# In each MLP's second pair, one block's products a step later; new issue times around both attention stages

## The chip, the cores and the metric

The kernel runs on one core of a Trainium2 chip. The metric is the device time of one execution in microseconds (us); the median of repeated runs counts. The engines are TensorE (PE; its weight loads are listed as PEld), VectorE (DVE), ScalarE (ACT), GpSimd (POOL) and SyncE (SP). SP computes nothing here: it issues DMAs, in the order in which they are written. POOL issues some DMAs too.

## What is computed

The reference is a trunk of two layers over 256 tokens of width 2048, all in float32. The parts that matter here:

```python
h = x
# layer A
u = rms_norm(h, a_norm_g);  q, k, v, fz = split(u @ a_w_in)     # 2048 x (3*2048 + 16)
h = h + forgetting_attention(norm(q), norm(k), v, log_sigmoid(fz + b_f)) @ a_w_out
h = h + relu(rms_norm(h, g) @ mlp_w1[0])**2 @ mlp_w2[0]         # 2048 x 8192, 8192 x 2048
# keys and values shared by the B layers, then layer B
k_sh, v_sh = split(rms_norm(h, kv_norm_g) @ kv_w)
q = norm(rms_norm(h, b_norm_g) @ b_w_q)
h = h + chunked_relbias_attention(q, norm(k_sh), v_sh, rel) @ b_w_out
h = h + relu(rms_norm(h, g) @ mlp_w1[1])**2 @ mlp_w2[1]
```

## The kernel before

**Products.** Nearly all time goes into products with weights. Every float32 weight block is split on the chip into a high part `hi` (a rounding copy on ACT, line 312) and a low part `lo` (a subtraction on DVE, line 313). A product of 512 columns is then three matmuls on PE: high by high (line 579), high weights by the low part of the activations (line 581), low weights by high (line 583). The third pass is the first that needs `lo`.

**Pairs, forms and own units.** The weights are cut into pairs. A pair has four corner blocks, "11", "12", "21" and "22", and instead of eight block products does seven, of the sums that Strassen's scheme wants. The program calls each of the seven a form; in order they are "11", T3 = 22 + 12, T2 = T3 + 11, T1 = 12 + 11, "21", T4 = T2 + 21, and "22". A form of the MLPs has two halves of 6 matmuls each. What the scheme leaves over are own units (`a2` to `a7`, `b2` to `b7`), ordinary pieces of weights with 12 matmuls each.

**Where the sums are made.** T3 and T2 are additions on DVE (`make`, line 937), each in two halves. T1 and T4 are accumulating DMAs issued by POOL (`put`, line 946): the new block is added in memory to a tile that holds the other term. `bring` (line 911, SP) loads the corner blocks. Tiles are named after what they hold: `raw` and `zraw` are pieces for own units, `w` a loaded corner of an MLP pair, `wT` the tile for T3, T2 and T4 in turn, `R` corners in the attention stages, `query` the T3 of the query projection.

**What sets the order.** The instruction order on each engine is the order of the program text; nothing reorders it. `TABLES["ORD"]` says for each kind of pair how own units and the last forms alternate after the first four forms: in "a4 F F a5 a6 a7 F b4" the three F are forms "21", T4 and "22" (that the fifth, sixth and seventh come in this order is `FO`, "456"). Tables with six entries (`W1F`, `W2F`, `QF` and so on) say how many own units ahead of a pair's start its loads of "12", "22", "21", "11" and its T3 and T1 are issued:

```python
for name, at in zip(("12", "22", "21", "11", "T3", "T1"), p.units):
    if d == at and p.deep and name == "T3":
        make(p, "T3", 0)
    elif d == at:
        (bring if name[0] != "T" else put if p.adds and name == "T1" else make)(p, name)
```

The second half of T3 follows one own unit later. `fetch` lets ACT and DVE split up to three units ahead of PE. Side work (softmax pieces, squares, sums, transposes, copies of rows) sits in a list of steps, `fill`; masks such as `HM` and `KM` say how many steps run after each unit of the attention stages, and `ATA`, `ATB`, `LONG`, `SHORT`, `KX`, `XOH`, `T0H` and the like into which step each piece is put.

**Ways of turning a result.** The output of a product is turned for the next one: DVE transposes 32 by 32 blocks into `z` (line 427), and then either `hop` copies 16 small blocks, eight DMAs on SP and eight on POOL (line 453, `q<-z`), or `carry` writes whole rows to DRAM (line 437, `turn<-z`) and reads them back with four DMAs (line 443, `q<-turn`). Of the tables `T`, `T0H` and `T0K` an entry of -1 in second place means `hop`.

**The order of stages.** Projection of layer A with its attention woven in, output projection, MLP A, which ends with the pairs of the query projection (`in_w_qb`, tables `QF` and `QS`), key and value projection with attention B, output projection, MLP B. In each MLP the pairs of the first matrix (`in_w1fa`, `in_w1fb`) and of the second (`in_w2fa`, `in_w2fb`) alternate after the first two; the "second pair" is the second of the first matrix, and a pair of the second matrix follows it.

Of the kernel before, what the change touches and what calls it, by code (L numbers as in the profile page):

```python
# [27 lines left out]
UN = 1024  # L28
AHEAD = 2
TABLES = {  # L30
    "ATA": ((11, 13, 15, 19, 10), (9, 12, 16, 18, 10), (8, 13, 15, 19, 9), (9, 9, 12, 12, 10)),
    "ATB": ((10, 13, 14, 18, 9), (9, 13, 15, 16, 11), (10, 12, 15, 17, 10), (7, 10, 12, 12, 9)),
# [13 lines left out]
    "LONG": ((0, 1, 2, 5, 9, 11, 11, 14, 14), (0, 0, 0, 4, 7, 9), (1, 0, 1, 3, 5, 5), (2, 0, 1, 2, 4, 5)),  # L46
    "OFH": (12, 8, 2, 7, 5, 5),
    "OFK": (11, 10, 5, 6, 8, 4),
    "ORD": {"deep1": "a4 F b4 F a5 F a6 a7", "qkv": "a2 a3 a4 F a5 F a6 F a7 b2 b3 b4", "ahead0": "F a4 F a5 a6 a7 F b4",
        "kv": "a2 F a3 a4 a5 F a6 a7 F b2 b3 b4", "deep0": "a4 F F F b4 a5 a6 a7", "ahead1": "a4 F F a5 a6 a7 F b4"},  # L50
    "OSH": (10, 11, 5, 6, 4, 2),
    "OSK": (8, 8, 6, 7, 4, 2),
    "OUTH": "F a2 a3 a4 a5 F b2 b3 F b4 G b5 G a6 a7 G b6 b7 G c2 G c3 G c4 c5 G c6 c7 d2 d3 d4",
    "OUTK": "a2 a3 F b2 a4 b3 F a5 F b4 b5 G G a6 a7 G b6 G c2 b7 G c3 G c4 c5 d2 G c6 c7 d3 d4",
    "QF": (4, 7, 1, 4, 2, 2),
    "QS": (10, 5, 4, 8, 3, 1),
    "SHORT": ((2, 0, 1, 4, 7, 7, 9, 9, 12), (2, 2, 3, 3, 7, 7, 8, 11, 13), (0, 1, 1, 4, 7, 7), (0, 0, 0, 2, 4, 4)),
# [13 lines left out]
    "XOH": (9, 12, 13, 10),  # L71
    "XOK": (9, 14, 12, 14),
    "XS": (2, 5, 4, 1),
}
EARLY = 3
LAZY = ("qkv", "kv", "out0", "out1")
# [3 lines left out]
DEEP = 2 * UN  # L80
WIDE1 = (1, 2, 3, 4, 5, 6, 7)
# [15 lines left out]
def trunk(ctx: ExitStack, tc: tile.TileContext, xT, xr, gs, hg, bf, wgate, w_in, w_oa, w1a, w1fa, w1sa, w2fa, w2sa,  # L97
          w_kv, w_qb, w_ob, w1b, w1fb, w1sb, w2fb, w2sb, rel, out):
    nc = tc.nc
    V, S, G, TE, SY = nc.vector, nc.scalar, nc.gpsimd, nc.tensor, nc.sync  # L100

    def pool(name, bufs, **kw):
        return ctx.enter_context(tc.tile_pool(name=name, bufs=bufs, **kw))
# [5 lines left out]
    qkv = pool("qkv", 2)  # L109
# [82 lines left out]
    def plan_mlp(w1, w1f, w1s, w2f, w2s, rest, when, more=None):  # L192
        pairs = []

        def add(w, wf, ws, i, wides, order, times, cols=WIDE):
            j = wides.index(i) if i in wides else i - sum(1 for k in wides if k < i)
            names = ("11", "12", "21", "22")
            if i in wides:
                m = 8 - cols // 512
                src = [[None] * (8 - m) + [ws[m * (2 * j + q) + u] for u in range(m)] for q in range(2)]  # L200
                big = {k: wf[4 * j + m] for m, k in enumerate(names)}
            else:
                src = [[w[16 * j + 8 * q + u] for u in range(8)] for q in range(2)]
                big = {k: src[int(k[1]) - 1][int(k[0]) - 1] for k in names}
            pairs.append(Pair(big, src, order, len(pairs) % 2 == 1, times, cols if i in wides else UN))

        rooms = {"12": "v0", "22": "k0", "11": "k1", "21": "v1"}
        seq = [(0, 0, 0), (0, 0, 1)]
        for c in range(NCH):
            seq += [(1, c, 0)] + [(0, c + 1, 0)] * (c + 1 < NCH) + [(1, c, 1)] + [(0, c + 1, 1)] * (c + 1 < NCH)  # L210
        for m, (second, c, q) in enumerate(seq):
            i = 2 * c + q
            if second:
                add(None, w2f, w2s, i, WIDE2, "deep%d" % q, TABLES["W2L" if i == 7 else "W2S" if q else "W2F"], DEEP)
            else:
                add(w1, w1f, w1s, i, WIDE1, "ahead%d" % q if i else "early", TABLES["W1E" + when] if not i else TABLES["W1I" + when] if i == 1 else TABLES["W1S" if q else "W1F"], DEEP)
            pairs[-1].at = second, c, q
        if more is not None:
            for q in range(2):
                add(more, None, None, q, (), "" if q else "query", TABLES["QS" if q else "QF"])  # L220
                pairs[-1].at = 1, NCH, q
        plan, rest = join(pairs, rooms, rest)
        return queue(plan + rest)

    def queue(plan):
        units.extend(Form(p, i, q == 3) if q > 1 else p.src[q][i] for p, q, i in plan)
        return plan

    def join(pairs, rooms, rest):
        plan = []  # L230
        for p in pairs:
            p.rooms = rooms
            if p.order != "early":
                rooms = {"12": rooms["11"], "22": rooms["12"], "11": rooms["21"], "21": rooms["22"]}
            mine, rest = p.plan(rest)
            plan += mine
        return plan, rest
# [33 lines left out]

    plan_h, rest, tail_h = plan_heads(w_in, "H", w_oa)
    plan_a = plan_mlp(w1a, w1fa, w1sa, w2fa, w2sa, rest, "H", w_qb)
    plan_k, rest, tail_k = plan_heads(w_kv, "K", w_ob)
    plan_b = plan_mlp(w1b, w1fb, w1sb, w2fb, w2sb, rest, "K")
    ready = deque()

# [118 lines left out]
    def room(tag, name, dtype=F32):  # L396
        return qkv.tile([P, DEEP], dtype, name=name, tag=tag, bufs=1)
# [72 lines left out]
    LONG, SHORT, SHORT2 = TABLES["LONG"], TABLES["SHORT"], TABLES["SHORT2"]  # L470
# [351 lines left out]
    early = room("bias", "early")  # L822
# [521 lines left out]
```

## Time and profile before

| | us |
|---|---|
| Median of 3 runs | 2069.12 |
| Lowest, highest | 2067.84, 2071.15 |
| The profiled execution | 2071.87 |
| Its span | 2070.1 |
| PE busy | 2050.1 (99%) |
| DVE busy | 1776.8 (86%) |
| ACT busy | 1398.8 (68%) |
| POOL busy | 243.9 (12%) |

PE executes 9068 matmuls. Times in the views are those of the one profiled execution, counted from the start of its span. In a timeline a row has the start, the duration, the engine, the line, the operation, output and inputs, how many instructions it groups, and in brackets how long the engine stood idle before it and what ended that. Instructions of one engine overlap a little, so that the distance of two starts is less than a duration.

### The profile page before, as it was taken

The numbers are of one execution on the slowest core, as the hardware profiler recorded it, in microseconds if no ns is written. First come the engines' busy times: TensorE is split into PE (matmuls) and PEld (weight loads), VectorE is DVE, ScalarE is ACT, GpSimd is POOL, SyncE is SP. The second block draws the span as 40 slices with busy tenths as digits, with TensorE's granted clock in tenths as the row PEclk, the third lists the DMA queues.
The fourth block names the chain that finished last, engine by engine and source line by source line (L and its number), as shares of the span: only waits on it lengthen the run. The fifth ranks groups of instructions, "written<-read, shape, count | busy, mean of one in ns | idle before, by whom it ended". The sixth has DMA issues, their size and how long they took to land.

```text
span 2070.1 us, 27097 instructions
## 1 busy us (share of the span) xinstructions
PE 2050.1 (99%) x9068; PEld 1689.7 (82%) x9068; DVE 1776.8 (86%) x2058; ACT 1398.8 (68%) x1799; POOL 243.9 (12%) x355
## 2 busy tenths in 40 slices
PE   9999999999999999999999999999999999999999
PEld 7888878878888888888888888888788888888887
DVE  6788788889899899899888678888998988988996
ACT  6766566667677677676778566667766675776764
POOL 1111010021101102101012011100211111111020
PEclk9999999999999999999999999999999999999999
DMA  9898888788889898897988888888888888888885
GB/s 328 258 278 273 265 262 268 281 263 256 284 270 284 252 299 274 243 286 251 285 253 262 290 260 265 256 264 284 277 284 270 267 267 286 259 284 260 288 261 148
DMA packets 174221, 556.20 MB, mean 269 GB/s; under 512 B 40688, under 2 KB 68992, under 8 KB 151040
## 3 DMA queue, kind: packets, MB, share of 16 engines
q1 hardware_dynamic: 153344, 463.94, 62.8%
q0 software_dynamic: 20448, 89.96, 21.9%
q8 instruction: 71, 1.16, 0.2%
q14 instruction: 70, 0.57, 0.1%
q10 hardware_dynamic: 288, 0.57, 0.1%
HBM read 514.50 MB, written 26.76 MB: 261 GB/s over the span
## 4 chain that ended last, share of the span: by engine, by line
PE 82%; DMA 6%; issue 5%; DVE 4%; ACT 1%; SPq 1%; POOL 0%; DVEq 0%; ACTq 0%; POOLq 0%
PE acc L579 19%; PE acc L583 19%; PE acc L581 19%; PE s L583 7%; PE s L579 7%; PE s L581 7%; DVE lo L313 2%; DMA wT<-in_w1fa 2%; ACT hi L312 1%; DMA raw<-in_w_in 1%; PE po L751 1%; DMA wT<-in_w1fb 1%; PE po L714 1%; DMA w<-in_w2fb 1%; DMA turn<-z 0%
## 5 line engine op out<-in xcount | busy, mean ns | idle before, releaser
L313 DVE TENSOR_TENSOR lo<-raw,hi 128x1024 fp32r<-128x1024 f32 (+1 forms) x414 | 500.0, 1212 | 94.6 <-ACT hi L312 86.2
L312 ACT ACTIVATE hi<-raw 128x1024 fp32r<-128x1024 f32 (+1 forms) x414 | 434.7, 1054 | 198.1 <-PE acc L581 134.2
L579 PE MATMUL acc<-hi,act 128*128 128x512 f32 x1784 | 500.1, 393 | 8.1 <-ACT hi L312 7.6
L583 PE MATMUL acc<-lo,act 128*128 128x512 f32 x1784 | 494.4, 390 | 1.3 <-DVE lo L313 1.0
L581 PE MATMUL acc<-hi,act 128*128 128x512 f32 x1784 | 493.8, 390 | 0.0
L579 PEld LDWEIGHTS acc<-hi,act 128*128 128x128 f32 x1784 | 333.4, 188 | 79.3 <-ACT hi L312 10.1
L583 PEld LDWEIGHTS acc<-lo,act 128*128 128x128 f32 x1784 | 334.1, 188 | 74.8 <-DVE lo L313 5.9
L581 PEld LDWEIGHTS acc<-hi,act 128*128 128x128 f32 x1784 | 335.3, 188 | 70.7 <-DVE act L370 0.5
L312 ACT ACTIVATE hi<-w 128x1024 fp32r<-128x1024 f32 x258 | 271.1, 1058 | 127.9 <-PE acc L581 86.5
L313 DVE TENSOR_TENSOR lo<-wT,hi 128x1024 fp32r<-128x1024 f32 x220 | 267.1, 1221 | 74.7 <-ACT hi L312 71.0
L313 DVE TENSOR_TENSOR lo<-w,hi 128x1024 fp32r<-128x1024 f32 x258 | 310.0, 1217 | 20.1 <-ACT hi L312 18.8
L312 ACT ACTIVATE hi<-wT 128x1024 fp32r<-128x1024 f32 x220 | 232.2, 1059 | 114.1 <-PE acc L581 51.8
L579 PE MATMUL s<-hi,act 128*128 128x512 f32 x530 | 146.4, 391 | 0.0
L583 PE MATMUL s<-lo,act 128*128 128x512 f32 x530 | 145.3, 389 | 0.7 <-DVE lo L313 0.7
L581 PE MATMUL s<-hi,act 128*128 128x512 f32 x530 | 144.8, 388 | 0.0
L453 POOL DMA_DIRECT2D q<-z x200 | 99.4, 512 | 251.8 <-DVE z L427 212.0
L583 PEld LDWEIGHTS s<-lo,act 128*128 128x128 f32 x530 | 99.0, 188 | 22.6 <-DVE lo L313 2.4
L581 PEld LDWEIGHTS s<-hi,act 128*128 128x128 f32 x530 | 99.4, 188 | 20.6
L579 PEld LDWEIGHTS s<-hi,act 128*128 128x128 f32 x530 | 99.1, 188 | 20.8 <-ACT hi L312 0.4
L579 PE MATMUL s<-hi,S 128*128 128x512 f32 x288 | 89.5, 392 | 0.0
L583 PE MATMUL s<-lo,S 128*128 128x512 f32 x288 | 88.9, 390 | 0.1
L581 PE MATMUL s<-hi,S 128*128 128x512 f32 x288 | 88.7, 389 | 0.0
(213 smaller groups left out, 2235.8 us busy)
## 6 DMA issues: line engine op xcount, KB each, us to landing
raw<-in_w_in SPq DMA_DIRECT2D x75, 512.0 KB, 5.8
w<-in_w2fa SPq DMA_DIRECT2D x32, 1024.0 KB, 6.4
w<-in_w2fb SPq DMA_DIRECT2D x32, 1024.0 KB, 6.2
w<-in_w1fa SPq DMA_DIRECT2D x28, 1024.0 KB, 7.2
w<-in_w1fb SPq DMA_DIRECT2D x28, 1024.0 KB, 7.0
raw<-in_w2sa SPq DMA_DIRECT2D x52, 512.0 KB, 7.7
raw<-in_w_kv SPq DMA_DIRECT2D x52, 512.0 KB, 5.2
raw<-in_w2sb SPq DMA_DIRECT2D x51, 512.0 KB, 7.0
```

The source lines that it names most:

```text
L312: S.activation(hi[:, c], raw[:, c], AF.Copy)
L313: V.tensor_tensor(lo[:, c], raw[:, c], hi[:, c].bitcast(F32), op=ALU.subtract)
L453: (G if i % 2 else SY).dma_start(dst[32 * j : 32 * j + 32, i * n : (i + 1) * n], z[32 * i : 32 * i + 32, j * n : (j + 1) * n])
L579: TE.matmul(ps[:, cols], xh, cut(hi, j), start=first, stop=False, **kw)
L581: TE.matmul(ps[:, cols], xl, cut(hi, j), start=False, stop=False, **kw)
L583: TE.matmul(ps[:, cols], xh, cut(lo, j), start=False, stop=last, **kw)
L714: TE.matmul(s[:, P : 3 * P], q[:, a, P:T], k[:, a], start=True, stop=True)
L751: TE.matmul(po[:, :T], v[:, 0, a * P : (a + 1) * P], pT[:, :2], start=True, stop=False)
```

## The change

The kind of the second pair changes from "ahead1" to a kind of its own, "second". The fifth own unit, `a5`, comes between form "21" and form T4 there, so T4's products are 12 matmuls later in PE's order. The tables for the attention stages, the pairs right behind them and the query projection get other numbers. The number of matmuls, splits and loads stays; one of the turned results (third entry of `T0K`) goes by `carry` instead of `hop`.

```diff
-        "kv": "a2 F a3 a4 a5 F a6 a7 F b2 b3 b4", "deep0": "a4 F F F b4 a5 a6 a7", "ahead1": "a4 F F a5 a6 a7 F b4"},
+        "second": "a4 F a5 F a6 a7 F b4"},
...
-    "QF": (4, 7, 1, 4, 2, 2),
+    "QF": (4, 4, 2, 3, 2, 1),
...
-    "W1IH": (11, 7, 6, 7, 3, 2),
+    "W1IH": (11, 7, 6, 9, 4, 1),
...
-                add(w1, w1f, w1s, i, WIDE1, "ahead%d" % q if i else "early", TABLES["W1E" + when] if not i else TABLES["W1I" + when] if i == 1 else TABLES["W1S" if q else "W1F"], DEEP)
+                add(w1, w1f, w1s, i, WIDE1, ("second" if i == 1 else "ahead%d" % q) if i else "early", TABLES["W1E" + when] if not i else TABLES["W1I" + when] if i == 1 else TABLES["W1S" if q else "W1F"], DEEP)
```

Because of one line more at the top of the file, line numbers after the change are higher by one.

On DVE, in MLP A's second pair, before: `wT_3816` holds T4, the `raw`, `zraw` and `raw` that follow it are `a5`, `a6` and `a7`; `wT_4141` is T3 of the next pair, `w_4071` and `w_4001` are that pair's "22" and "12", and `w_3713` is the second pair's "22".

```order
L313 TENSOR_TENSOR lo<-wT_3816,hi 128x1024 x2
L313 TENSOR_TENSOR lo<-raw,hi 128x1024
L313 TENSOR_TENSOR lo<-zraw,hi 128x1024
L313 TENSOR_TENSOR lo<-raw,hi 128x1024
L937 TENSOR_TENSOR wT_4141<-w_4071,w_4001 128x1024
L313 TENSOR_TENSOR lo<-w_3713,hi 128x1024
```

The same place after (T4 is now in `wT_3798`, the next pair's T3 in `wT_4113`, the second pair's "22" in `w_3715`):

```order
L314 TENSOR_TENSOR lo<-raw,hi 128x1024
L314 TENSOR_TENSOR lo<-wT_3798,hi 128x1024 x2
L938 TENSOR_TENSOR wT_4113<-w_4071,w_4001 128x1024
L314 TENSOR_TENSOR lo<-zraw,hi 128x1024
L314 TENSOR_TENSOR lo<-raw,hi 128x1024
L314 TENSOR_TENSOR lo<-w_3715,hi 128x1024
```

The subtraction for `a5` now stands ahead of T4's two, and the first half of the next pair's T3 stands right behind them, ahead of the subtractions for `a6` and `a7` instead of behind them. MLP B has the same order at its second pair.

On SP, at the end of MLP A, before: `w_8744`, `w_8883` and `w_8885` are "22", "12" and "11" of the first pair of the query projection.

```order
L437 DMA turn<-z 128x1024
L911 DMA w_8744<-in_w_qb 128x1024
L291 DMA raw<-in_w2sa 128x1024
L443 DMA q<-turn 32x4x256 x4
L291 DMA raw<-in_w2sa 128x1024
L437 DMA turn<-z 128x1024
L291 DMA zraw<-in_w2sa 128x1024
L911 DMA w_8883<-in_w_qb 128x1024
L911 DMA w_8885<-in_w_qb 128x1024
L291 DMA raw<-in_w2sa 128x1024
L443 DMA q<-turn 32x4x256 x4
```

The same place after: `w_8881` and `w_8883` are "12" and "22", `w_8939` is "11".

```order
L438 DMA turn<-z 128x1024
L292 DMA zraw<-in_w2sa 128x1024
L912 DMA w_8881<-in_w_qb 128x1024
L912 DMA w_8883<-in_w_qb 128x1024
L292 DMA raw<-in_w2sa 128x1024
L444 DMA q<-turn 32x4x256 x4
L912 DMA w_8939<-in_w_qb 128x1024
```

"22" is now issued with "12", and "11" stands behind the four reads of `turn`, which were behind it.

On DVE, in attention A near the start of the kernel, before: `row`, `pbuf` and `t` belong to the softmax, and `acc<-acc,p_980` combines two accumulators of a pair.

```order
L734 RECIPROCAL row<-row 128x2
L736 TENSOR_SCALAR pbuf<-pbuf,row 128x128
L736 TENSOR_SCALAR pbuf<-pbuf,row 128x256
L427 STREAM_TRANSPOSE pbuf<-pbuf 128x3x4x32
L723 SCALAR_TENSOR_TENSOR t<-po,cq,nb 128x128
L725 TENSOR_REDUCE row<-t 128x1
L723 SCALAR_TENSOR_TENSOR t<-po,cq,nb 128x256
L725 TENSOR_REDUCE row<-t 128x1
L976 SCALAR_TENSOR_TENSOR acc<-acc,p_980 128x512
L313 TENSOR_TENSOR lo<-R,hi 128x1024
```

The same place after:

```order
L977 SCALAR_TENSOR_TENSOR acc<-acc,p_980 128x512
L314 TENSOR_TENSOR lo<-R,hi 128x1024
L735 RECIPROCAL row<-row 128x2
L737 TENSOR_SCALAR pbuf<-pbuf,row 128x128
L737 TENSOR_SCALAR pbuf<-pbuf,row 128x256
L428 STREAM_TRANSPOSE pbuf<-pbuf 128x3x4x32
L724 SCALAR_TENSOR_TENSOR t<-po,cq,nb 128x128
L726 TENSOR_REDUCE row<-t 128x1
L724 SCALAR_TENSOR_TENSOR t<-po,cq,nb 128x256
L726 TENSOR_REDUCE row<-t 128x1
```

The combining step and the split of the next `R` now come ahead of the eight softmax instructions. Some 150 us later, also in attention A, the first addition for T3 of a pair (`wT<-R`) stands four subtractions earlier.

More of the change, by code (lines that the diff above doesn't have):

```diff
@@ L30 @@
 TABLES = {
-    "ATA": ((11, 13, 15, 19, 10), (9, 12, 16, 18, 10), (8, 13, 15, 19, 9), (9, 9, 12, 12, 10)),
-    "ATB": ((10, 13, 14, 18, 9), (9, 13, 15, 16, 11), (10, 12, 15, 17, 10), (7, 10, 12, 12, 9)),
[1 row of a table removed]
+    "ATA": ((11, 13, 15, 19, 9), (9, 12, 16, 18, 11), (8, 13, 15, 19, 9), (9, 9, 12, 12, 10)),
+    "ATB": ((10, 13, 14, 18, 9), (9, 13, 15, 17, 11), (9, 12, 15, 17, 10), (7, 10, 12, 12, 9)),
[1 row of a table added]
     "GS": (1,),
[11 rows of a table removed]
[L46 to L49, printed above, removed]
-        "kv": "a2 F a3 a4 a5 F a6 a7 F b2 b3 b4", "deep0": "a4 F F F b4 a5 a6 a7", "ahead1": "a4 F F a5 a6 a7 F b4"},
[L51 to L54, printed above, removed]
-    "QF": (4, 7, 1, 4, 2, 2),
-    "QS": (10, 5, 4, 8, 3, 1),
-    "SHORT": ((2, 0, 1, 4, 7, 7, 9, 9, 12), (2, 2, 3, 3, 7, 7, 8, 11, 13), (0, 1, 1, 4, 7, 7), (0, 0, 0, 2, 4, 4)),
[1 row of a table removed]
[11 rows of a table added]
+    "LONG": ((0, 1, 2, 5, 9, 10, 11, 14, 14), (0, 0, 0, 4, 7, 9), (1, 0, 1, 2, 5, 5), (1, 0, 1, 4, 5, 5)),
+    "OFH": (11, 10, 1, 7, 7, 7),
+    "OFK": (10, 9, 4, 9, 8, 4),
[3 rows of a table added]
+    "OSH": (7, 9, 7, 5, 5, 1),
+    "OSK": (9, 7, 4, 7, 5, 1),
+    "OUTH": "F a2 a3 b2 a4 a5 b3 b4 F G F G b5 a6 a7 G b6 b7 G c2 G c3 G d2 c4 c5 G c6 c7 d3 d4",
+    "OUTK": "a2 a3 F b2 a4 F b3 a5 F b4 b5 G G a6 a7 G b6 G c2 b7 d2 G c3 G c4 c5 c6 G c7 d3 d4",
+    "QF": (4, 4, 2, 3, 2, 1),
+    "QS": (10, 4, 4, 8, 3, 1),
+    "SHORT": ((4, 0, 0, 3, 6, 8, 8, 9, 12), (2, 2, 3, 3, 7, 7, 8, 10, 13), (2, 0, 0, 2, 6, 7), (0, 0, 0, 2, 4, 5)),
[1 row of a table added]
     "T": ((1, -1, 5, 14, 14, 14, 15, 20, 20), (0, 2, 8, 10, 10, 14, 18, 20, 22), (0, -1, 5, 6, 7, 7), (0, -1, 4, 5, 5, 5)),
[4 rows of a table removed]
[4 rows of a table added]
     "W1F": (7, 5, 1, 5, 4, 3),
[2 rows of a table removed]
[2 rows of a table added]
     "W1S": (8, 6, 4, 5, 4, 1),
     "W2F": (6, 5, 1, 5, 4, 3),
[1 row of a table removed]
[1 row of a table added]
     "W2S": (7, 7, 4, 5, 3, 1),
-    "XOH": (9, 12, 13, 10),
+    "XOH": (9, 12, 13, 11),
     "XOK": (9, 14, 12, 14),
-    "XS": (2, 5, 4, 1),
+    "XS": (0, 5, 6, 2),
 }
```

38 rows, old and new, of the table TABLES are left out of this document.

## The prediction

> **What bounds the kernel now.** I read the busy times first, then what PE waited for, then the timelines around each wait. The first row is from the page, the others from the waits of PE (total us, times, longest us).
>
> ```profile
> PE 2050.1 (99%) x9068; PEld 1689.7 (82%) x9068; DVE 1776.8 (86%) x2058; ACT 1398.8 (68%) x1799; POOL 243.9 (12%) x355
> PE acc L579 <- ACT hi L312: 7.6, 6, 3.4
> PE acc L583 <- DVE lo L313: 2.6, 3, 1.2
> ```
>
> PE sets the end, and a change that keeps all matmuls can win only PE's waits (2070.1 - 2050.1, 20 us at most, the start included) and slow matmuls. The longest wait, 3.4 us, is at T4 of MLP A's second pair. PE's timeline there, then its clock, then two pieces of the chain of waits:
>
> ```profile
> 442.21 0.92 PE L579 MATMUL acc<-hi,act 128*128 128x512 f32 x2 [3.37 <-ACT hi L312]
> 446.65 1.09 PE L579 MATMUL acc<-hi,act 128*128 128x512 f32 x4
> ```
>
> ```profile
> 400.00:450.00 50.00, 46.58 (x196) 37.23 (x195) 39.11 (x40) 32.12 (x37) 9.74 (x18) 0.97 0.88 287
> ```
>
> ```profile
> 448.65 0.91 PE acc L583 x4
> 468.68 0.73 PE acc L583 x2
> ```
>
> Four matmuls take 0.91 us later on, 0.2275 each, so the two halves of T4, 12 matmuls, should take 2.73. From 442.21 to 446.65 they take 4.44: after the wait they run slowly, at a cost of 1.71, and the granted clock (0.97) is the trace of it. Wait and slowness make 5.08 us. ACT was waiting for POOL's accumulating DMA; POOL's and ACT's rows:
>
> ```profile
> 426.83 0.92 POOL L946 DMA_DIRECT2D wT<-in_w1fa  x1 [2.69 <-DVE lo L313]
> 441.10 2.01 ACT L312 ACTIVATE hi<-wT 128x1024 fp32r<-128x1024 f32 x2 [4.48 <-DMA wT<-in_w1fa]
> ```
>
> MLP B has the same place, with less of it and no slow matmuls behind it:
>
> ```profile
> 1465.34 0.73 PE L579 MATMUL acc<-hi,act 128*128 128x512 f32 x2 [1.18 <-ACT hi L312]
> 1481.81 1.20 PE L583 MATMUL s<-lo,act 128*128 128x512 f32 x4 [0.37 <-DVE lo L313]
> ```
>
> **The second pair of MLP A.** The put's place does not move, so T4 is ready at 442.21 again. PE is free at 442.21 - 3.37 = 438.84, does `a5` until 441.57, and waits 0.64 instead of 3.37; the slow stretch goes. Gross, 5.08 - 0.64 = 4.4 us.
>
> What is late next is the following pair. Its T3 now stands on DVE directly behind T4's two subtractions, and needs that pair's "22", which SP issues only behind a hop. SP's rows, and the landing of the loads in both MLPs (first A, then B):
>
> ```profile
> 431.61 10.69 SPq L453 DMA_DIRECT2D q<-z  x8
> 442.41 1.00 SPq L911 DMA_DIRECT2D w<-in_w2fa  x2
> DMA to landing us min/median/max: 4.9/5.8/6.7
> ```
>
> ```profile
> 1464.44 0.83 SPq L911 DMA_DIRECT2D w<-in_w2fb  x2
> DMA to landing us min/median/max: 5.0/6.0/7.0
> ```
>
> And DVE's timeline in MLP A:
>
> ```profile
> 442.19 2.36 DVE L313 TENSOR_TENSOR lo<-wT,hi 128x1024 fp32r<-128x1024 f32 x2 [2.84 <-ACT hi L312]
> 444.47 1.22 DVE L313 TENSOR_TENSOR lo<-raw,hi 128x1024 fp32r<-128x1024 f32 x1
> ...
> 448.62 1.22 DVE L937 TENSOR_TENSOR wT<-w,w 128x1024 f32<-128x1024 f32 x1
> ...
> 452.51 1.23 DVE L313 TENSOR_TENSOR lo<-w,hi 128x1024 fp32r<-128x1024 f32 x1 [0.36 <-ACT hi L312]
> ...
> 458.94 1.23 DVE L313 TENSOR_TENSOR lo<-w,hi 128x1024 fp32r<-128x1024 f32 x1 [0.53 <-ACT hi L312]
> ...
> 467.41 1.22 DVE L313 TENSOR_TENSOR lo<-wT,hi 128x1024 fp32r<-128x1024 f32 x1
> ```
>
> Before, "22" lands at 442.41 + 4.9 = 447.3 and T3 starts at 448.62, 1.3 later: it waits for nothing. After, DVE is through with T4 at 444.47 and stands 2.8 us until 447.3. Behind it are queued the subtractions for `a6` and `a7` and all else on DVE. A subtraction occupies 1.14 (two from 442.19 to 444.47), T3's half as much, so `a6` has its `lo` at about 447.35 + 2.3 = 449.6. PE comes out of T4 at 441.57 + 0.64 + 2.73 = 444.94 and does the 8 matmuls of `a6` that need no `lo` (1.82) until 446.8: it waits 2.8 to 2.9. So much of the 4.4 is gone again.
>
> The rest goes to DVE itself. T3 starts 1.27 earlier than before, but two subtractions (2.28) that stood ahead of it now stand behind it, so that DVE is 1.0 later from there on. Two gaps of before, 0.36 and 0.53, fill up. At 467.41 DVE is where it was, 0.1 later; and at 468.68 PE's third pass starts as soon as this `lo` is there. Whatever PE has won since 442 is lost there. Net: 0, with bounds of -0.5 (another such gap does not fill) and +2.8 (no wait for "22").
>
> Whether the new wait makes matmuls slow again can be read between two rows: 3.37 did, 1.18 did not, and 2.85 is nearer the first. By the row, up to 1.7 us of slowness at `a6`. The Trainium skill ("TensorE: Matmul & The Clock Gate", Part 1, What's actually happening) gives half clock after an idle window of about 3.4 us that runs free; the trace agrees, and by that rule a wait of 2.85 would mostly stay fast. By the one reading or the other the sum is the same, because PE would otherwise wait at 468.68 in any case.
>
> **The second pair of MLP B.** DVE's timeline:
>
> ```profile
> 1465.32 2.36 DVE L313 TENSOR_TENSOR lo<-wT,hi 128x1024 fp32r<-128x1024 f32 x2 [1.34 <-ACT hi L312]
> 1467.60 3.49 DVE L313 TENSOR_TENSOR lo<-raw,hi 128x1024 fp32r<-128x1024 f32 x3
> ...
> 1472.21 1.22 DVE L937 TENSOR_TENSOR wT<-w,w 128x1024 f32<-128x1024 f32 x1
> ...
> 1480.58 1.18 DVE L313 TENSOR_TENSOR lo<-raw,hi 128x1024 fp32r<-128x1024 f32 x1
> ```
>
> T4 is ready at 1465.34, and PE with `a5` until 1465.34 - 1.18 + 2.73 = 1466.9, so the wait of 1.18 goes. "22" lands at 1464.44 + 5.0 = 1469.4; DVE is free at 1467.60 and stands 1.8. `a5`'s subtraction (1.14) fell into DVE's idle time ahead of 1465.32, so DVE ends the stretch 0.7 later than before, and it has no gap in it. PE waits about 0.4 at `a6`, and what is left is eaten by DVE's being late. Net: 0, with bounds of -0.7 and +1.55 (1.18 + 0.37, no wait for "22").
>
> **Attention A.** PE's rows at two waits and DVE's at what is moved:
>
> ```profile
> 107.05 0.70 PE L579 MATMUL acc<-hi,S 128*128 128x512 f32 x2 [1.13 <-ACT pbuf L731]
> 279.39 0.73 PE L583 MATMUL acc<-lo,act 128*128 128x512 f32 x2 [0.99 <-DVE lo L313]
> 282.32 1.19 PE L583 MATMUL s<-lo,act 128*128 128x512 f32 x4 [0.35 <-DVE lo L313]
> ```
>
> ```profile
> 106.22 0.69 DVE L976 SCALAR_TENSOR_TENSOR acc<-acc,p 128x512 f32<-128x512 f32 x1
> ...
> 264.86 1.22 DVE L937 TENSOR_TENSOR wT<-R 128x1024 f32<-128x1024 f32 x1
> ```
>
> The first wait is put down to a softmax step, but PE starts at 107.05, when DVE's combination at 106.22, which reads the accumulator that PE writes next, is over. It stood behind eight softmax instructions; it now stands ahead of them, so I take the whole 1.1 (bounds 0 and 1.13; the softmax then comes later, but its results are used units later). Before 279 and 282 DVE is busy without a gap; T3's half, 1.14 as above, at 264.86, moves ahead of this stretch: 1.1 of 1.34 (bounds 0 and 1.34). Together +2.2.
>
> **The query projection.** SP's two rows, then the landing of its three loads, then DVE and PE:
>
> ```profile
> 1019.00 0.81 SPq L911 DMA_DIRECT2D w<-in_w_qb  x2
> ...
> 1023.44 1.75 SPq L443 DMA_DIRECT2D q<-turn  x4
> ```
>
> ```profile
> DMA to landing us min/median/max: 5.8/6.9/8.0
> ```
>
> ```profile
> 1031.72 1.22 DVE L313 TENSOR_TENSOR lo<-w,hi 128x1024 fp32r<-128x1024 f32 x1
> ```
>
> ```profile
> 1044.90 0.73 PE L583 MATMUL acc<-lo,S 128*128 128x512 f32 x2 [1.20 <-DVE lo L313]
> ```
>
> "11" was issued by 1019.8 and is now moved past the four reads of `turn`, to 1025.2. It lands at 1032.1 by the median, ACT's rounding copy takes it to 1033.2, and DVE, which started on it at 1031.72, stands 1.5 with all that is behind. DVE then sets PE's start at 1044.90, so I take -1.5 (0.4 to 2.6 by the shortest and longest landing; 0 if the lateness of DVE was already covered). "22", now issued at 1019, lands by 1027 for an addition at 1033, and costs nothing.
>
> **The remaining tables.** PE waits for nothing else there that these could remove. The `carry` in place of one `hop` I put at 0: a later reading could cost a wait of the 1.5 kind, and nothing waits there now, so nothing can be won.
>
> **Sum.** 2.2 - 1.5 + 0 + 0 = 0.7 us less. The profiled execution took 2071.87 (span 2070.1), 2.75 above the median of 2069.12, or 0.13%; the terms are alike for either, so 2069.12 - 0.7 = 2068.4. What a measurement of this kernel can tell from no change is about 0.2%, 4.1 us.
>
> **Rivals.**
>
> 1. Faster: T3 does not wait, because "22" is there. For it speaks that the hop ahead of it took 10.69 us to issue in MLP A and 6.33 in MLP B:
>
> ```profile
> 1456.74 6.33 SPq L453 DMA_DIRECT2D q<-z  x8
> ```
>
>    With 4 us less, "22" would land at 443. Then MLP A keeps 2.8 and MLP B up to 1.55: 2068.4 - 4.35 = 2064.0. Against it: nothing that the hop waits for is moved by the new order.
>
> 2. Slower: "22" lands later than in this profile, and each us beyond 447.3 and 1469.4 costs one, since DVE has no gap left. Other loads of 1 MB took longer; the loads at 397 and at 1424 landed, counted from their issue, after:
>
> ```profile
> DMA to landing us min/median/max: 7.5/9.6/12.9
> ```
>
> ```profile
> DMA to landing us min/median/max: 9.3/10.5/11.8
> ```
>
>    With 7.5 in both MLPs, 2.6 and 2.5 are added: 2068.4 + 5.1 = 2073.5. From a lateness of 4.8 in all it is slower than can be told from before. Against it: at these two places 4.9 and 5.0 were measured, and the new order adds no DMA beside them.
>
> 3. The change does not do what it says: the put goes out later, because its T2 comes later, and T4 still stalls for 3.4 us with slow matmuls. Then MLP A is as before and so is the sum, 2068.4. The order speaks against it: the put stays behind the same instructions.
>
> **How the numbers follow.** The forecast, in which each pair gives back what it gains, has 0.46, with the third rival in it; its own range is 2065 to 2071.5 (attention between 0 and 2.5, query between 0 and -2.6, the pairs at -1.2 to +1). The first rival has 0.32: half of its gain may come from one MLP, but attention may give its upper bounds. The second has 0.22, with the query stage at its worst. So faster 0.32, same 0.46, slower 0.22. The range takes in the first rival with a further 1.5 of attention and query (2062.5) and the second with 0.5 (2074.0).
>
> **What would show it.** Right: T4's wait in MLP A under 1 us and no slow matmuls behind it; DVE idle ahead of T3 by 2 to 3 us in A and 1 to 2 in B, released by the load of "22"; a new PE wait at `a6` of 2 to 3 us in A; PE's wait near 468 longer than before; no wait near 107; a wait of 2 to 3 at the query stage. Wrong: T3 without idle time ahead of it, or new waits of PE over 1 us where I name none.

## The result and the profile after

| | before | after |
|---|---|---|
| Median, us | 2070.39 (10 runs) | 2065.22 (10 runs) |
| Lowest, highest, us | 2064.83, 2072.06 | 2063.25, 2067.49 |
| The profiled execution, its span, us | 2071.87, 2070.1 | 2064.13, 2062.3 |

The ratio is 0.998, 95% interval 0.997 to 0.9989: 2 to 6 us less. The forecast was 2068.4 in a range of 2062.5 to 2074.0, with "faster by over 4.1 us" as the second likeliest case. It took 0.7 us off the 2069.12 of before's first three runs; by the medians of ten runs each, 5.2 came off. The two profiled executions are 7.7 us apart, so a part of what the traces show is chance of one execution.

The page's busy times and PE's waits after (total us, times, longest us):

```profile
PE 2049.0 (99%) x9068; PEld 1690.6 (82%) x9068; DVE 1777.8 (86%) x2058; ACT 1400.1 (68%) x1799; POOL 238.5 (12%) x347
PE acc L584 <- DVE lo L314: 3.3, 7, 1.1
PE acc L580 <- ACT hi L313: 1.8, 3, 0.7
PE s L584 <- DVE lo L314: 1.1, 2, 0.7
PE acc L580 <- ACT act L408: 0.7, 1, 0.7
```

The waits for `hi` fell from 7.6 to 1.8 us, those for `lo` rose from 2.6 to 3.3 with output `acc` and from 0.7 to 1.1 with output `s`, and one of 0.7 for activations is new. All waits of PE together fell from some 15 to 9. In MLP A, PE's timeline around T4 and `a6`, and the window that answers to 400:450 of before:

```profile
437.44 1.19 PE L584 MATMUL acc<-lo,act 128*128 128x512 f32 x4 [0.67 <-DVE lo L314]
438.47 0.63 PE L580 MATMUL acc<-hi,act 128*128 128x512 f32 x2
...
444.24 1.19 PE L584 MATMUL acc<-lo,act 128*128 128x512 f32 x4 [1.06 <-DVE lo L314]
```

```profile
396.00:446.00 50.00, 48.21 (x211) 38.84 (x210) 39.90 (x42) 33.47 (x38) 9.77 (x18) 1.00 0.92 290
```

T4 (438.47) starts without a wait of its own; 0.67 falls on `a5`'s third pass just ahead of it. The clock is 1.00. DVE and SP at the same place:

```profile
437.30 2.35 DVE L314 TENSOR_TENSOR lo<-wT,hi 128x1024 fp32r<-128x1024 f32 x2
441.82 1.22 DVE L938 TENSOR_TENSOR wT<-w,w 128x1024 f32<-128x1024 f32 x1 [2.17 <-DMA w<-in_w2fa]
...
461.79 1.22 DVE L314 TENSOR_TENSOR lo<-wT,hi 128x1024 fp32r<-128x1024 f32 x1
```

```profile
427.72 8.85 SPq L454 DMA_DIRECT2D q<-z  x8
436.69 0.99 SPq L912 DMA_DIRECT2D w<-in_w2fa  x2
```

DVE stands 2.17 us ahead of T3, released by the load of "22", as forecast, and `a6` then waits 1.06. MLP B shows the same, with DVE's and PE's rows:

```profile
1463.67 1.23 DVE L938 TENSOR_TENSOR wT<-w,w 128x1024 f32<-128x1024 f32 x1 [2.00 <-DMA w<-in_w2fb]
```

```profile
1427.55 1.20 PE L580 MATMUL acc<-hi,act 128*128 128x512 f32 x4 [0.67 <-ACT act L408]
...
1466.09 1.19 PE L584 MATMUL acc<-lo,act 128*128 128x512 f32 x4 [0.37 <-DVE lo L314]
...
1475.30 1.19 PE L584 MATMUL s<-lo,act 128*128 128x512 f32 x4 [0.74 <-DVE lo L314]
```

The first of these rows is the new wait for activations, at the start of MLP B. In attention A, DVE's combination and PE's rows:

```profile
103.45 0.70 DVE L977 SCALAR_TENSOR_TENSOR acc<-acc,p 128x512 f32<-128x512 f32 x1 [0.49 <-PE acc L584]
```

```profile
105.97 0.62 PE L580 MATMUL acc<-hi,S 128*128 128x512 f32 x2
...
279.85 1.19 PE L584 MATMUL s<-lo,act 128*128 128x512 f32 x4 [0.34 <-DVE lo L314]
```

The combination ends 1.8 us before PE needs it; there is no wait at 105.97, and of the two near 280 one is left.

**PE's lead by stretch.** All kernels here execute 9068 matmuls, so the start of the n-th matmul in before's trace less the start of the n-th in another kernel's trace is PE's lead there. The n-th is not always the same product: besides the second pair, the new `OUTH`, `OUTK` and the entries "qkv" and "kv" of `ORD` are orders too, so the lead is read where such a stretch is over. The table has what is won (+) or lost (-) of it per stretch, in us. The stretches end, on before's time, at 426 (just ahead of T4 in MLP A), 447 (in T4's products), 492, 1076 (the query stage included), 1346 (attention B), 1451 (just ahead of T4 in MLP B), 1469, 1510 and the end. One execution of each kernel:

```
                    to426   447   492  1076  1346  1451  1469  1510   end    sum
after                +3.9  +4.3  -3.4  +2.1  +0.1  -1.2  +1.7  -2.1  +2.0   +7.5
order_alone          -2.9  +4.3  -4.9  +1.4  +0.2  -1.4  +1.8  -5.0  +2.3   -4.3
tables_alone         +4.0  +2.8  -0.1  -0.5  +0.2  -2.1  -0.6  +0.4  +2.1   +6.2
first_half           +5.6  -1.0  -0.2  +1.7  -0.4  -0.3  -0.6  -0.0  +0.7   +5.5
second_half          -1.8  +0.1  -0.0  +0.9  -0.0  -3.6  -0.8  +0.4  +2.3   -2.5
old_query_times      +4.3  +4.3  -2.3  +1.0  +0.6  -1.1  +1.5  -2.2  +1.8   +7.8
late_t3              +1.5  +4.3  -1.9  -0.1  +0.3  -4.2  +1.3  -0.5  +1.6   +2.4
late_t3_early_row    +3.6  +4.3  -1.1  +1.8  +0.1  -4.4  +1.6  -0.5  +1.7   +7.1
first_half_late_t3   +5.8  +4.3  -1.1  +1.7  -1.1  -5.6  +1.8  -1.1  +2.4   +7.1
late_t3_both_rows    +5.9  +4.3  -1.2  +2.3  +0.3  +0.1  +1.8  -0.5  +1.2  +14.2
order_late_t3        -0.0  +5.1  -2.4  -0.4  -0.3  -1.2  +1.8  -1.1  +2.0   +3.5
```

The last stretch gains 0.7 to 2.4 in every kernel, also where nothing is changed there, most of it at one wait that before's profiled execution has:

```profile
1745.63 0.70 PE L579 MATMUL acc<-hi,Sh 128*128 128x512 f32 x2 [1.37 <-DVE acc L976]
```

With what lies around it, this is some 1.7 us of the 7.5 that is chance: order_alone and order_late_t3, which have before's instructions there, win the same 1.7. The first 90 us hold chance too: the leads there are -0.7 to +1.0 (-0.2 in the changed kernel, +1.0 in first_half), and -0.7 to +0.2 in the three kernels that have before's instructions up to T4.

### The profile page after: what moved, and what is told of

It reads as the page before. It is cut to its first block, busy times and chain, and to the rows that moved or that the text cites. A ratio compares the mean times of both kernels' runs of the same rounds, so it can differ in the third digit from the quotient of the medians.

```text
span 2062.3 us, 27087 instructions
## 1 busy us (share of the span) xinstructions
PE 2049.0 (99%) x9068; PEld 1690.6 (82%) x9068; DVE 1777.8 (86%) x2058; ACT 1400.1 (68%) x1799; POOL 238.5 (12%) x347
## 4 chain that ended last, share of the span: by engine, by line
PE 87%; DMA 5%; issue 4%; DVE 2%; ACT 1%; SPq 0%; POOL 0%; DVEq 0%; ACTq 0%; POOLq 0%
PE acc L584 20%; PE acc L582 20%; PE acc L580 20%; PE s L584 8%; PE s L580 8%; PE s L582 8%; DMA q<-turn 1%; DVE lo L314 1%; DMA q<-z 1%; DMA turn<-z 1%; PE po L715 1%; PE po L752 1%; DMA wT<-in_w1fb 1%; DMA wT<-in_w1fa 1%; DVE z L428 0%
```

## Experiments

Names stand for kernels; times are medians, and ratios are to before in the same session, with their 95% intervals. The changed kernel was not timed again beside these kernels, so it is compared with them by its ratio to before, 0.998 (0.997 to 0.9989). Code is shown in cuts, some of them parts of a line.

**order_alone**, **tables_alone**: which part of the change brings the gain. The first is before with

```diff
-"ahead%d" % q if i else "early"
+("second" if i == 1 else "ahead%d" % q) if i else "early"
```

and the row "second" in `ORD` and `FO`; the second is the changed kernel with this undone, and with before's `W1IH` and `W1IK`.

> Before's tables, with only the order of the second pair changed (a5 ahead of T4's products). The prediction's theory: T4's wait in MLP A falls from 3.4 to under 1 us and the slow matmuls go, but DVE stands 2 to 3 us ahead of the next pair's T3 until its 22 lands, and what PE has won (4 to 4.5) is down to 0 to 1 us some 40 us later; MLP B likewise ends at -0.7 to +0.7. In all 0 to 1 us less than before. Rival: the order brings the whole measured gain, 4 to 6 us less than before, and PE's lead stays.

> The new tables with the old order of the second pair (and its two old rows of issue times, which belong to that order). The prediction's theory, with its sizes mended by the trace after: attention A and what lies around it give 3 to 4 us, the query stage 0 to 1, the rest -1 to 0; T4's wait of about 3 us in MLP A and its slow matmuls are there as before. In all 3 to 5 us less than before. Rival (the order brings the gain): 0 to 1 us less than before.

Measured: order_alone 2073.60 (12 runs), ratio 1.0008 (0.9994 to 1.0021); tables_alone 2064.13 (12 runs), ratio 0.9963 (0.995 to 0.9977). The gain is the tables'; no gain of the order beside them shows. In order_alone the order does in MLP A what was forecast: T4's products are 4.3 earlier, and 4.9 are lost again behind them. DVE's and PE's rows there:

```profile
445.17 2.36 DVE L313 TENSOR_TENSOR lo<-wT,hi 128x1024 fp32r<-128x1024 f32 x2 [1.73 <-ACT hi L312]
450.63 1.23 DVE L937 TENSOR_TENSOR wT<-w,w 128x1024 f32<-128x1024 f32 x1 [3.10 <-DMA w<-in_w2fa]
```

```profile
453.04 1.73 PE L583 MATMUL acc<-lo,act 128*128 128x512 f32 x4 [2.67 <-DVE lo L313]
454.58 1.91 PE L579 MATMUL acc<-hi,act 128*128 128x512 f32 x4
456.28 1.37 PE L581 MATMUL acc<-hi,act 128*128 128x512 f32 x4
```

T3's wait is 3.10 (2.8 was worked out) and `a6`'s 2.67 (2.85), and the matmuls behind it are slow. In MLP B the pair ends at -3.2 (1.8 - 5.0), where -0.7 was the worst that was forecast. DVE's and PE's rows there:

```profile
1473.62 1.23 DVE L937 TENSOR_TENSOR wT<-w,w 128x1024 f32<-128x1024 f32 x1 [2.51 <-DMA w<-in_w2fb]
```

```profile
1476.03 1.21 PE L583 MATMUL acc<-lo,act 128*128 128x512 f32 x4 [1.17 <-DVE lo L313]
1486.71 1.26 PE L583 MATMUL s<-lo,act 128*128 128x512 f32 x4 [2.18 <-DVE lo L313]
```

DVE stands 2.51, where 1.8 was worked out, and has no gap from then to the second of PE's waits, behind which matmuls are slow.

In tables_alone T4 waits with the old order, but for 1.8 where about 3 was expected, and no slow matmuls follow:

```profile
436.62 0.73 PE L580 MATMUL acc<-hi,act 128*128 128x512 f32 x2 [1.80 <-ACT hi L313]
```

**first_half**, **second_half**: which tables. Before with only layer A's rows (`ATA`, `HF`, `HM`, `HS`, `OFH`, `OSH`, `OUTH`, `SHORT`, `T0H`, `W1EH`, `XOH`, `XS`, "qkv"), and with only the others (without `W1IH`, `W1IK` and the order).

> Before's kernel with the new tables of layer A's side alone (attention A, its output projection, MLP A's first pair and first turned results); order of the second pair and all of layer B's side as before. Theory now: attention A brings 2.5 to 4 us by PE position 304 (1.4 at the wait near 107, 1.5 near 279, 0.6 near 288), and T4's accumulating DMA in MLP A lands within 13 us of its issue instead of 14.2, so that its wait is 1.8 or less and no slow matmuls follow (2.8 more). In all 5 to 7 us less than before, with no new wait at the start of MLP B. Rival: T4's sooner landing hangs on tables of the other side or on chance, and only the 2.5 to 4 remain.

> Before's kernel with the new tables of layer B's side and of the query projection alone. Theory now: nothing gained, a wait of 0.5 to 2 us of PE at the start of MLP B for the activations (ACT behind the reads of turn), 0 to 1 us gained at the query stage: 0 to 2 us more than before. Rival: part of the measured gain comes from here, 1 to 3 us less than before.

Measured: first_half 2065.92 (10 runs), ratio 0.9979 (0.9968 to 0.999); second_half 2068.95 (12 runs), 0.9998 (0.9986 to 1.001). Layer A's rows alone bring a gain, and its place is ahead of T4: +5.6 by 426, or 4.5 counted from 90 on. The others alone bring none that shows. tables_alone, with both, has the lower ratio, but its interval overlaps first_half's. In second_half's trace the wait that was expected at the start of MLP B is absent; the 3.6 that are lost up to 1451 go at a wait of 0.94 near 1393 and behind 1430. Of the step at DVE's combination, 1.15 are won between 96 and 124, where the order of the matmuls agrees again, in every kernel with the new `HM`, and -0.03 or -0.02 in every one without, so that term is sized. The rest of the expectation for first_half fell: T4's put takes 14.2 us from issue to ACT's start, as in before, and T4's wait is back:

```profile
421.18 0.93 POOL L946 DMA_DIRECT2D wT<-in_w1fa  x1 [1.99 <-DMA q<-z]
435.42 2.00 ACT L312 ACTIVATE hi<-wT 128x1024 fp32r<-128x1024 f32 x2 [4.34 <-DMA wT<-in_w1fa]
436.52 1.22 PE L579 MATMUL acc<-hi,act 128*128 128x512 f32 x2 [3.23 <-ACT hi L312]
```

tables_alone, with the same instructions up to there, had its `hi` 13.0 us after the issue (422.53 to 435.51), and first_half_late_t3 13.0 too. So the landing of this DMA differs by over 1 us with nothing changed ahead of it. Over the twelve traces it is 13.0 to 14.3 us in the seven kernels with before's `W1IH` and 11.9 to 12.6 in the five with its new entries for T3 and T1; the changed kernel has 12.6:

```profile
422.68 0.93 POOL L947 DMA_DIRECT2D wT<-in_w1fa  x1 [1.57 <-DMA q<-z]
435.29 2.01 ACT L313 ACTIVATE hi<-wT 128x1024 fp32r<-128x1024 f32 x2 [1.60 <-DMA wT<-in_w1fa]
```

No run changes this row alone, so it is not shown that the row is the cause, and what sets the rest was not found. The new order makes PE safe from it: T4's start waits 0.5 us at most in every trace of a kernel that has it.

**old_query_times**: the changed kernel with

```diff
-    "QF": (4, 4, 2, 3, 2, 1),
+    "QF": (4, 7, 1, 4, 2, 2),
```

> The changed kernel with the old issue times of the first pair of the query projection (22 three own units earlier, 11 one earlier and ahead of the reads of turn). The prediction's theory (11 behind the reads makes DVE late by 1.5): 1 to 1.5 us less than the changed kernel at this stage. Rival, from the trace after (11 landed in time and DVE did not stand for it): no difference, -0.4 to +0.4 at PE's wait near 1038.

Measured: 2064.91 (12 runs), against 2065.22 for the changed kernel. By the intervals, no difference shows. PE's wait at this place is 1.04 with the old times and 0.36 with the new, but 0.35 to 1.08 over all traces with the new. So the step of 1 to 1.5 that the prediction's theory asked for does not come, and the rival holds.

**late_t3**: the changed kernel with T3 and T1 of the pair behind the second pair one own unit later.

```diff
-    "W2F": (6, 5, 1, 5, 4, 3),
+    "W2F": (6, 5, 1, 5, 4, 3), "W2I": (6, 5, 1, 5, 3, 2),
...
-TABLES["W2L" if i == 7 else "W2S" if q else "W2F"]
+TABLES["W2L" if i == 7 else "W2S" if q else "W2F" if c else "W2I"]
```

> The changed kernel, with T3 and T1 of the pair behind the second pair one own unit later, so that T3 no longer stands ahead of a6's subtraction on DVE. If the wait for 22 costs what the new order won: DVE's 2 us of standing in each MLP and PE's wait of 1.1 at a6 go, and 1 to 3 us of the lead stay: 1 to 3 us less than the changed kernel. Rival (DVE is full in that stretch whatever the order, or T1 comes late now): 0 to 0.5 less, or up to 2 more, with a new wait at T1's products.

Measured: 2063.69 (12 runs), ratio 0.9962 (0.9949 to 0.9975). The stretch behind T4 loses 1.9 instead of 3.4 in MLP A and 0.5 instead of 2.1 in MLP B, DVE does not stand for T3, and `a6` does not wait. What is lost there even so goes in MLP A at waits of 0.54 and 0.40 near 463, for `Sh` and `lo`. The time is only 1.5 us under the changed kernel's, and the intervals of the two ratios overlap, so the gain is shown by the traces and not by the times. In the traced execution waits for activations that the changed kernel hardly has are large, 2.00 at the start of MLP A and 2.02 at that of MLP B. PE at the start of MLP A, the clock there, and SP:

```profile
405.41 1.47 PE L580 MATMUL acc<-hi,act 128*128 128x512 f32 x4 [2.00 <-ACT act L408]
406.67 2.07 PE L582 MATMUL acc<-hi,act 128*128 128x512 f32 x4
```

```profile
404.00:412.00 8.00, 6.59 (x21) 4.97 (x22) 7.31 (x7) 4.30 (x6) 0.87 (x1) 0.79 0.91 350
```

```profile
386.85 0.33 SPq L912 DMA_DIRECT2D w<-in_w1fa  x1
387.23 1.08 SPq L292 DMA_DIRECT2D raw<-in_w1a  x2
388.54 3.04 SPq L444 DMA_DIRECT2D q<-turn  x4
```

The reads of `turn` that bring MLP A's last activations stand behind the 1 MB of the second pair's "11", which the changed `W1IH` issues at 9 own units instead of 7.

**late_t3_early_row**, **late_t3_both_rows**: late_t3 with "11" at 7 in MLP A, then in both MLPs.

```diff
-    "W1IH": (11, 7, 6, 9, 4, 1),
+    "W1IH": (11, 7, 6, 7, 4, 1),
...
-    "W1IK": (11, 7, 3, 9, 4, 3),
+    "W1IK": (11, 7, 3, 7, 4, 3),
```

> The changed kernel with T3 of the pair behind the second pair one unit later, and block 11 of MLP A's second pair at 7 own units instead of 9, that is behind the reads of turn instead of ahead of them. Theory: the wait of 0.3 to 2 us of PE near 405 for the activations, seen with 9, is gone, since 1 MB less lies ahead of these reads; 0.5 to 2 us less than the same kernel with 9 (late_t3) by the lead of PE behind 410. Rival: the wait near 405 is chance of the DMAs and appears here too.

> The kernel late_t3_early_row with block 11 of the second pair at 7 own units instead of 9 in MLP B too. Theory: the wait of 2 us of PE at the start of MLP B (near 1428, for the activations behind the reads of turn) falls to 0 to 0.5, and PE's loss there of about 4 us against before to 0 to 2; the time is 1 to 3 us under late_t3_early_row's. Rival: the reads are slow there for another reason, and nothing changes.

Measured: 2060.31 (6 runs), ratio 0.9957 (0.9943 to 0.9971), and 2058.68 (6 runs), ratio 0.9953 (0.994 to 0.9967). With the row of MLP A the wait near 405 is gone; the one in MLP B is there, 2.06 with 3.8 us of lead lost, and with both rows it is gone too: +0.1 in the stretch to 1451 instead of -4.4. late_t3_both_rows is faster than both kernels of this case. Its interval lies clear of the changed kernel's, but overlaps that of tables_alone, which has the old order. That all of the gain comes from the rows is not shown: the waits at these places vary from trace to trace with the same row (with 9, in MLP A none, 0.28 and 2.00, in MLP B 0.54, 0.67, 2.02 and 2.06).

**first_half_late_t3**: first_half with the new order and `W2I`.

> The tables of layer A's side alone, plus the new order of the second pair with T3 of the following pair one unit later. If the order is worth something once T3's wait is out of its way: PE's lead behind MLP A's second pair is 1 to 2 us larger than with the tables of layer A's side alone, and 1 us larger behind MLP B's. Rival: T4's put lands in time with the new tables anyhow and DVE is full there, so that the lead is the same within 1 us.

Measured: 2063.65 (6 runs), ratio 0.9965 (0.9953 to 0.9978), against first_half's 2065.92. Through MLP A's second pair it wins 3.2 (4.3 - 1.1), where first_half loses 1.2; in MLP B 0.7 against -0.6. By the traces the order is worth something once T3 is out of its way, more than expected in MLP A, because first_half's T4 wait was nearly as long as before's. By the times it is less sure: the two intervals overlap, and late_t3 (0.9962) is no faster than tables_alone (0.9963), whose T4 waited 1.8. Of the 5.6 that first_half_late_t3 loses up to 1451, 4.0 go at one wait of 1.98 near 1346, for softmax rows read back from `turn`, and slow matmuls behind it; no other trace has this wait.

**order_late_t3**: order_alone with `W2I`.

> Before's tables with the new order of the second pair, and T3 and T1 of the pair behind it one unit later, nothing else. Theory (the order is worth something, and T3's wait for 22 takes it back): PE's lead over the order alone grows by 2 to 3 us behind MLP A's second pair and by 1 to 3 behind MLP B's; against before 2 to 5 us less. Rival (DVE is full there in any case): within 1 us of the order alone, that is no gain against before.

Measured: 2070.57 (11 runs), ratio 0.9997 (0.9986 to 1.0008); order_alone had 2073.60. The later T3 gives 3 us over the order alone by medians of two sessions, whose intervals overlap, and by the lead 3.3 in MLP A (2.7 against -0.6) and 3.9 in MLP B (0.7 against -3.2). Against before 2 to 5 us were expected and nothing shows in the time, though the two pairs win 3.4 against before's trace; before's T4 wait in its other executions is not known, so this stays open.

## Why the prediction was right or wrong

**T4's wait and the slow matmuls in MLP A: right.** 4.4 gross were forecast; 4.3 came, in order_alone too. The small wait that was left stood not at T4 but on `a5`'s third pass just ahead of it in the changed kernel (0.67, where 0.64 was worked out for T4).

**T3's wait for "22": right in kind and size.** Forecast 2.8 of standing and 2.85 at `a6`; the order alone showed 3.10 and 2.67. In the changed kernel it was 2.17 and 1.06, because the hop's issue took 8.85 instead of 10.69, so that "22" went out 1.8 earlier against PE. The net of the pair was +0.9 instead of 0. late_t3 and order_late_t3 showed the cause by taking the wait away. That DVE's being full takes the rest came in part: where the wait is gone, 1.1 to 2.4 are still lost behind T4.

**MLP B: right in the changed kernel** (-0.4 net for 0), too kind for the order alone (-3.2; the bound was -0.7). There DVE stood longer than worked out (2.51 for 1.8), its being late brought a second wait of 2.18, and the slow matmuls behind such a wait were not counted.

**Attention A: right in kind, the term too small.** 2.2 were forecast. From 90 to 426 the changed kernel won 4.1, and the others with the new tables and no long wait near 405 won 3.8 to 4.9. The combination gave the 1.15 that was put at 1.1. The step near 280 was put at 1.1 and gave 1.9 to 2.4 against before's trace; up to 1.2 behind 345 were not in the sum at all. Some of this is before's own spread: near 280 the three kernels with before's instructions stand at -2.2, -0.9 and +0.7 against it.

**The query stage: wrong.** The step "it lands at 1032.1, and DVE stands 1.5" failed. It took the reads of `turn` to be issued when they were before. Before's rows for `turn` in the chain of waits, then SP's, ACT's and DVE's rows after:

```profile
1014.94 8.43 DMA turn<-z
```

```profile
1008.58 0.34 SPq L438 DMA_DIRECT2D turn<-z  x1
...
1013.09 1.87 SPq L444 DMA_DIRECT2D q<-turn  x4
1015.00 0.47 SPq L912 DMA_DIRECT2D w<-in_w_qb  x1
```

```profile
1023.38 1.06 ACT L313 ACTIVATE hi<-w 128x1024 fp32r<-128x1024 f32 x1 [0.99 <-DMA w<-in_w_qb]
```

```profile
1024.92 1.22 DVE L314 TENSOR_TENSOR lo<-w,hi 128x1024 fp32r<-128x1024 f32 x1
```

At this place PE's lead is 6, so 1015.0 is 1021 on before's time, where 1025.2 was forecast. The rows of `turn` were written within 4.5 us (1008.58 to 1013.09), not 8.4, and the reads could start sooner. The moved issue times did this themselves: the write took 9.0 in old_query_times, which differs from the changed kernel in `QF` alone, and over the twelve traces 8.3 to 9.0 with the old `QF`, whose "22" is issued ahead of this write, and 4.0 to 5.5 with the new, which issues it behind. ACT waited 0.99 for the block, and DVE, busy with other blocks, not at all. PE's wait, 1.20 before, shrank where one of 2 to 3 had been named:

```profile
1037.97 0.73 PE L584 MATMUL acc<-lo,S 128*128 128x512 f32 x2 [0.36 <-DVE lo L314]
```

With -1.5 set to 0, and attention at the 3.9 of PE's lead at 426, the sum would have been 2069.12 - 3.9 = 2065.2. That this is the measured median is luck: the 3.9 are one execution's, and ten runs put before at 2070.39.

**The remaining tables at 0: wrong.** The prediction named no price for the 1 MB that `W1IH` moved ahead of the reads of `turn` at the start of MLP A, and none for MLP B's start, where 1.2 are lost in the changed kernel. In late_t3 waits of 2.00 and 2.02 stood at these two places.

**The rivals.** The first (T3 does not wait, 2064.0) gave about the time that came, by luck: its condition, a shorter hop, came in part (8.85), but T3 did wait, and the gain came from the tables. Of the second, DVE's having no gap left was seen in order_alone. The third did not occur.

## What to carry to other kernels

When products are moved to hide one transfer, read in the order what each engine behind the moved instruction now waits for: here an addition came to stand where its load had not landed, and on an engine that goes in order this gap cost most or all of what had been won. Move that instruction along, and look at every load that passes a small read on the same queue: with these two repairs the median went from 2065.2 to 2058.7, and the ratio to before from 0.998 to 0.9953. Size a gain from more than one trace where the wait hangs on DMAs: waits of 0.3 and 2.0 us stood at the same place in kernels with the same instructions there.

## What the runs showed of the hardware

A PE wait of about 2 us is enough for slow matmuls, where the prediction weighed 1.18 against 3.37 and took 2.85 as open. After waits of 1.88, 1.98, 2.00, 2.02, 2.06, 2.18, 2.67, 2.96, 3.23 and 3.37 us 6 to 13 of the next matmuls took some 0.43 us each instead of 0.23, at a cost of about 1.5 to 2.7 us; after 1.79, 1.80, 1.82 and 1.84 they did not (waits in the first 10 us left aside). The granted clock over 8 us around the wait of 2.00 was 0.79. The Trainium skill ("TensorE: Matmul & The Clock Gate", Part 1, What's actually happening) puts the idle window at about 3.4 us; the waits here disagree with that as a lower bound.
